# Delta net: z from PSUM by Silu, decays and key factors on ScalarE, masks on GpSimd, half of z behind the inverse's levels

## The chip, the cores and the metric

The kernel runs on one core of one Trainium2 chip. The metric is device time in microseconds from the start to the end of one execution, the median of several runs. TensorE's clock has two levels, 1.2 and 2.4 GHz; the trace gives the granted clock as 0.50 and 1.00.

## The reference

The program is a network of several layers for 256 tokens of width 1024 in fp32. The change is in its first layer, a gated delta net with 8 heads of 128:

```python
def gated_deltanet(hn, w_in, conv_w, a_log, dt_bias, out_norm_g, w_out):
    proj = hn @ w_in
    qkv = jax.nn.silu(causal_depthwise_conv(proj[..., :3 * DN_DIM], conv_w))
    z = proj[..., 3 * DN_DIM:4 * DN_DIM]
    ...
    o = chunk_gated_delta_rule(q, k, v, g, beta)
    o = rmsnorm(o, out_norm_g) * jax.nn.silu(z.reshape(b, t, DN_HEADS, DN_HEAD_DIM))
    return o.reshape(b, t, DN_DIM) @ w_out
```

Inside the chunked rule, with gc the running sum of the gates within a chunk:

```python
    decay = jnp.exp(jnp.where(tri_incl, gc[..., :, None] - gc[..., None, :], -jnp.inf))
    a_low = jnp.where(tri_strict, jnp.einsum('bhncd,bhnsd->bhncs', k_beta, k) * decay, 0.0)
    sol = lax.linalg.triangular_solve(a_mat, rhs, left_side=True, lower=True, unit_diagonal=True)
    attn_intra = jnp.einsum('bhncd,bhnsd->bhncs', q, k) * decay
    k_dec = k * jnp.exp(gc[..., -1:] - gc)[..., None]
```

The scan over chunks then makes the outputs from u, w, the decayed q and k, and attn_intra. The layers behind (an MLP, a block attention, the branch layer, its feed-forward) are the same in both kernels.

## The kernel before

A chunk here is 128 tokens, so there are 2 chunks (c) and 2 groups of 4 heads (g): four blocks (g, c), each a tile of 128 x 4 x 128. A scheduler puts every instruction into its engine's queue by priority in the order of the code; `later(n)` adds n to the priority of what stands under it, and `after(x)` (`tc.issue_after`) puts what stands under it behind instruction x on the same engine. Every engine works its queue in order.

Projections (`lin`, `group`) go in pieces of 512 columns: four weight tiles `wr` of 128x1024 come by DMA on SyncE's queue, ScalarE makes the rounded half `wh` (line 76) and VectorE the rest `wl` (line 56), and TensorE makes 96 matmuls of 128x128 on 128x256 in three passes (xh with wh, xl with wh, xh with wl) into two of the two `acc` banks of PSUM. The six other banks are `ps`. There are 4 buffers of `wr` and 5 of `wh` and `wl` each.

`delta_net` goes through these stages:

- `gates` makes beta and the running sums `gc`; `decays(g, c)` makes m = exp(-|row sum - gc|) for each block and for c = 1 the factors `qd`.
- `project` makes k, then q and vt: `conv_pair` copies the accumulator into a padded tile `pad` (its three leading columns are zeroed by GpSimd each time, line 507), starts y on ScalarE, adds three taps on VectorE (`cy`, line 59), and applies Silu.
- `unit_keys` and `gram` make the blocks of A from k, beta and m.
- `inverses`: the 32x32 diagonal blocks of A go through DRAM (`ga`, line 573; `at`, line 576; both issued by GpSimd) into a layout in which VectorE solves all of them in 31 steps of two instructions (`tmp`, `zt`). The result goes through DRAM again (`gz`, line 594; `Z`, line 597).
- `level_64` and `level_128`, each for four blocks, join the 32x32 inverses to 64x64 and then 128x128. Each has transposes (`turned`, line 603, called T below), a product with A ("Z,A"), ScalarE's copy `Y`, a product with X ("Y,X") and ScalarE's copy back into Z.
- `intra` multiplies m with the triangular mask `tri`, makes q times k ("kq" below) and multiplies it with m; for c = 1 it makes q times `qd`.
- `tokens(g)` transposes k and v, and VectorE makes kx and bv; `outputs(g)` makes u0, nw, S, vn and the outputs, normalises them and multiplies with z; the projection out follows.
- `on_z` makes Silu of z without a Silu table: a max, Exp, Ln(1+x), Exp, and a product with z and the norm's gain `onorm`. z comes in two pieces, columns 3072 to 3583 ("z0") and 3584 to 4095 ("z1").

`pin` is the load of ScalarE's table of Exp and Ln, placed behind the last Silu; what needs it stands behind it by `issue_after(pin.ins)`. Before, q and vt are written behind the levels in the code, but they and z have no need of Z and fill TensorE while VectorE works at the inverse. kq stands behind the levels, and the tokens behind kq.

Of the kernel before, what the change touches and what calls it, by code (L numbers as in the profile page):

```python
# [8 lines left out]
F32 = mybir.dt.float32  # L9
F32R = mybir.dt.float32r  # L10
I32 = mybir.dt.int32
AF = mybir.ActivationFunctionType
OP = mybir.AluOpType
# [3 lines left out]
P = 128  # L17
T = 256
D = 1024
KD = D // P  # L20
# [4 lines left out]
class Net:  # L25
# [420 lines left out]
    def delta_net(self):  # L446
        nc, tc, a = self.nc, self.tc, self.a
        W = a["dn_w_in"][0]
        H, d = 8, 128
        banks = self.ctx.enter_context(ExitStack())  # L450
        banks.enter_context(self.banks(2))
        with ExitStack() as ctx:
            dp = ctx.enter_context(tc.tile_pool(name="dn", bufs=1, reuse_waits="tile"))
# [45 lines left out]
            A = core.tile([P, 16, P], F32, name="A")  # L499
            Z = core.tile([P, 16, P], F32, name="Z")  # L500
            nc.gpsimd.memset(Z, 0.0)
            four = lambda t, g, c: t[:, (g * 2 + c) * 4:(g * 2 + c) * 4 + 4, :]

            def conv_pair(col, o, dst, behind):
                t = col // P
                pad = dp.tile([P, 2, T + 3], F32, tag="pad", name="pad", bufs=2)
                nc.gpsimd.memset(pad[:, :, 0:3], 0.0)
                self.copy(pad[:, :, 3:], o)
                y = dp.tile([P, 2, T], F32, tag="cy", name="cy", bufs=2)
                w = lambda j, i: cw[:, j * 24 + t + i:j * 24 + t + i + 1]  # L510
                for i in range(2):
                    self.act(y[:, i, :], o[:, i, :], AF.Copy, scale=w(3, i))
                for j in range(3):
                    for i in range(2):
                        self.stt(y[:, i, :], pad[:, i, j:j + T], w(j, i), y[:, i, :], OP.mult, OP.add)
                with self.after(*behind):
                    self.last_silu = self.act(dst, y, AF.Silu)
# [14 lines left out]

            def decays(g, c):

                h4 = slice(g * 4, g * 4 + 4)
                p = self.ps()
                mm4(p, lambda i: (gt[:, c, g * 4 + i:g * 4 + i + 1].to_broadcast([P, P]), self.tri[:, 0:P]))
                m = M[g, c] = big("m", 4)
                self.tt(m, v4(p), tok(gc[:, c, h4]), OP.subtract)
                if c == 1:  # L540
                    qd[g] = big("qd", 2)
                    self.last_exp = self.act(qd[g], v4(p), AF.Exp)
                self.act(m, m, AF.Abs)
                self.last_exp = self.act(m, m, AF.Exp, scale=-1.0)

            def unit_keys(g):
# [52 lines left out]
            def turned(zz):  # L599
                X = big("X", 2)  # L600
                p = self.ps()
                for i in range(4):
                    nc.tensor.transpose(p[:, i * P:(i + 1) * P], zz[:, i, :], self.ident)  # L603
                self.copy(X, v4(p))
                return X

# [32 lines left out]
            def intra(g, c):  # L639

                cs = slice(c * P, (c + 1) * P)
                m = M[g, c]
                self.tt(m, m, b4(self.tri[:, 0:P]), OP.mult)
                p = self.ps()
                mm4(p, lambda i: (k[g][:, i, cs], q[g][:, i, cs]))
                self.tt(m, v4(p), m, OP.mult)
                if c == 1:
                    self.tt(qd[g], q[g][:, :, cs], qd[g], OP.mult)

            def tokens(g):  # L650

                h4 = slice(g * 4, g * 4 + 4)
                for c in range(2):
                    cs = slice(c * P, (c + 1) * P)
                    p = self.ps()
                    for i in range(4):
                        nc.tensor.transpose(p[:, i * P:(i + 1) * P], k[g][:, i, cs], self.ident)
                    kx[c] = big(f"kx{c}", 1, late)
                    self.tt(kx[c], v4(p), tok((beg if c else kdec)[:, h4]), OP.mult)
                    p = self.ps()  # L660
                    for i in range(4):
                        nc.tensor.transpose(p[:, i * P:(i + 1) * P], vt[g][:, i, cs], self.ident)
                    bv[c] = big(f"bv{c}", 1, late)
                    self.tt(bv[c], v4(p), tok(beta[:, c, h4]), OP.mult)
# [6 lines left out]
            def outputs(g):  # L671
                Z0, Z1 = four(Z, g, 0), four(Z, g, 1)
                p = self.ps()
                mm4(p, lambda i: (Z0[:, i, :], bv[0][:, i, :]))
                u0 = big("u0", 1, late)
                self.copy(u0, v4(p))
                p = self.ps()
                mm4(p, lambda i: (kx[1][:, i, :], Z1[:, i, :]))
                nw = big("nw", 1, late)
                self.act(nw, v4(p), AF.Copy, scale=-1.0)  # L680
                yield
                p = self.ps()
                mm4(p, lambda i: (kx[0][:, i, :], u0[:, i, :]))
                S = big("S", 1, late)
                self.copy(S, v4(p))
                yield
                p = self.ps()
                for i in range(4):
                    o = p[:, i * P:(i + 1) * P]
                    self.mm(o, Z1[:, i, :], bv[1][:, i, :], i == 0, False)  # L690
                    self.mm(o, nw[:, i, :], S[:, i, :], False, True)
                vn = big("vn", 1, late)
                self.copy(vn, v4(p))
                for j in range(2):
                    yield
                    p = self.ps()
                    for i in (2 * j, 2 * j + 1):
                        o = p[:, (i % 2) * T:(i % 2) * T + T]
                        self.mm(o[:, 0:P], u0[:, i, :], M[g, 0][:, i, :], i % 2 == 0, True)
                        self.mm(o[:, P:T], S[:, i, :], qd[g][:, i, :], False, False)  # L700
                        self.mm(o[:, P:T], vn[:, i, :], M[g, 1][:, i, :], False, True)
                    o = self.pairs(p)
                    sq = self.sq_pair(o)
                    q2 = late.tile([P, 2, T], F32, tag="q2", name="q2", bufs=1)
                    self.act(q2, q[g][:, 2 * j:2 * j + 2, :], AF.Square, scale=math.sqrt(d * d * EPS))
                    self.tt(sq, sq, q2, OP.add)
                    zj = z[:, g * 4 + 2 * j:g * 4 + 2 * j + 2, :]
                    self.tt(zj, o, zj, OP.mult)
                    p = self.ps()
                    self.mm(p, self.ones, sq, True, True)  # L710
                    r = dp.tile([P, 2, T], F32, tag="kr", name="kr", bufs=1)
                    self.rsqrt_wide(r, self.pairs(p), d, oeps)
                    self.tt(zj, zj, r, OP.mult)
                    h2 = slice(2 * j, 2 * j + 2)
                    self.split(xo[g][0][:, h2, :], xo[g][1][:, h2, :], zj)

            def on_z(col, o):
                h = col // P - 24
                zj = z[:, h:h + 2, :]
                e = dp.tile([P, 2, T], F32, tag="ze", name="ze", bufs=1)  # L720
                self.ts(e, o, -80.0, None, OP.max)
                with tc.issue_after(pin.ins):
                    self.act(e, e, AF.Exp, scale=-1.0)
                self.act(e, e, AF.Ln, bias=1.0)
                self.act(e, e, AF.Exp, scale=-1.0)
                self.stt(zj, o, self.vec["onorm"], e, OP.mult, OP.mult)

            both = [(g, c) for g in range(2) for c in range(2)]
            gates()
# [11 lines left out]
            with tc.tile_pool(name="inv", bufs=1, reuse_waits="tile") as sv:  # L741
                inverses(sv)
            late = ctx.enter_context(tc.tile_pool(name="late", bufs=1, reuse_waits="tile"))
            for level in (level_64, level_128):
                for g, c in both:
                    level(four(A, g, c), four(Z, g, c))
            project(q, "q", 0, 0, behind)
            project(q, "q", 0, 1, behind)
            project(vt, "vt", 2048, 0, behind)
            project(vt, "vt", 2048, 1, behind)  # L750
            pin = self.table(self.last_silu)
            for g, c in both:
                intra(g, c)
            tokens(0)
            step = lambda it: next(it, None)
            out = [outputs(g) for g in range(2)]
            step(out[0])
            with self.later(300):
                self.lin(W, KD, [(3072, 512)], rd, on_z)
            step(out[0])  # L760
            step(out[0])
            xo[0] = (late.tile([P, 4, T], F32R, name="xoh"), late.tile([P, 4, T], F32R, name="xol"))
            with self.later(600):
                self.lin(W, KD, [(3584, 512)], rd, on_z)
            xo[1] = self.new_xg(0)
            tokens(1)
            for _ in range(6):
# [798 lines left out]
```

## Time and profile before

| | us |
|---|---|
| median of 3 runs | 1304.6 (1304.56 to 1306.42) |
| the profiled execution | 1307.26 |
| its span | 1305.5 |
| TensorE busy in the span | 1256.2 (96%) |
| VectorE, ScalarE, GpSimd busy | 866.9, 738.9, 21.1 |
| mean granted clock | 0.974 |

All times in the rows are microseconds from the start of the span, unless they are marked ns. A row of a stretch gives the busy time of each engine with its instructions, the granted clock (PEclk) and the DMA's share. The mean of a group is the modelled duration of one instruction; in a queue without waits the next begins a little before that end. A matmul's modelled duration holds its pipeline, so its price is the distance from start to start.

### The profile page before, as it was taken

To read this page: it belongs to the slowest core of one execution; us is meant where nothing else is said; L and a number is where in the kernel's file an instruction comes from. 1 tells how busy PE (TensorE), PEld (TensorE's weight loads), DVE (VectorE), ACT (ScalarE), POOL (GpSimd) and SP (SyncE) were. 2 spreads that over 40 slices of the span, in tenths; PEclk is the share of its full clock that TensorE was granted. 3 is DMA by queue.
4 is the path that set the end of the run, shared out by engine and by line. 5 is a ranking of instruction groups with operands and counts; after the bars stand their busy time and mean duration, and the time that the engine had idled before them with its cause. 6 is when DMAs were issued, how large, how long until landed. Compare 5 with 4: busy or idle time off the path is not lost.

```text
span 1305.5 us, 23759 instructions
## 1 busy us (share of the span) xinstructions
PE 1256.2 (96%) x9666; PEld 1198.3 (92%) x9666; DVE 866.9 (66%) x1385; ACT 738.9 (57%) x1126; POOL 21.1 (2%) x68
## 2 busy tenths in 40 slices
PE   7997789999999999999999999999999998999998
PEld 6997688999999999999999988799999997999997
DVE  6799236754546665744545998998556685877775
ACT  6874435654545445854545755665447565656554
POOL 2010100000000000000000000000000000000000
PEclk8998678999999999999999999999999999999999
DMA  6454302766664744656662563446564654465552
GB/s 208 136 170 146 81 1 85 238 199 184 180 191 142 216 144 146 210 163 189 180 184 78 163 178 98 145 133 192 184 187 148 206 164 129 132 207 172 183 177 83
DMA packets 99633, 207.32 MB, mean 159 GB/s; under 512 B 9694, under 2 KB 12292, under 8 KB 99524
## 3 DMA queue, kind: packets, MB, share of 16 engines
q1 hardware_dynamic: 98114, 202.85, 50.7%
q0 software_dynamic: 928, 2.88, 0.9%
q8 instruction: 76, 1.25, 0.4%
q14 instruction: 33, 0.27, 0.1%
q10 hardware_dynamic: 482, 0.08, 0.0%
HBM read 204.21 MB, written 1.57 MB: 158 GB/s over the span
## 4 chain that ended last, share of the span: by engine, by line
PE 83%; DVE 8%; ACT 3%; DMA 2%; issue 2%; POOL 0%; SPq 0%; ACTq 0%; DVEq 0%; POOLq 0%
PE acc L53 50%; PE ps L53 31%; DVE wl L56 2%; DVE yc L59 1%; ACT wh L76 1%; PE ps L603 1%; DVE cy L59 1%; PE ps L893 1%; DVE tmp L56 1%; DVE zt L56 0%; DVE sq L56 0%; DMA wr<-in_w_xkv_dram 0%; DMA Z<-gz 0%; DMA xt<-in_x_dram 0%; DMA gz<-zt 0%
## 5 line engine op out<-in xcount | busy, mean ns | idle before, releaser
L56 DVE TENSOR_TENSOR wl<-wr,wh 128x1024 fp32r<-128x1024 f32 (+1 forms) x384 | 466.5, 1219 | 304.3 <-ACT wh L76 303.3
L76 ACT ACTIVATE wh<-wr 128x1024 fp32r<-128x1024 f32 (+1 forms) x384 | 402.7, 1053 | 393.0 <-PE acc L53 241.7
L53 PE MATMUL acc<-xh,wh 128*128 128x256 f32 (+1 forms) x1064 | 306.8, 289 | 7.2 <-DVE z L59 5.2
L53 PE MATMUL acc<-xh,wl 128*128 128x256 f32 (+1 forms) x1064 | 305.7, 288 | 3.5 <-DVE wl L56 3.5
L53 PE MATMUL acc<-xl,wh 128*128 128x256 f32 (+1 forms) x1064 | 305.1, 287 | 0.8 <-DVE xl L56 0.8
L53 PE MATMUL ps<-xh,wh 128*128 128x256 f32 (+1 forms) x872 | 247.9, 285 | 6.2 <-ACT xh L69 3.5
L53 PE MATMUL ps<-xl,wh 128*128 128x256 f32 (+1 forms) x872 | 247.6, 284 | 0.5 <-DVE xl L56 0.3
L53 PE MATMUL ps<-xh,wl 128*128 128x256 f32 (+1 forms) x872 | 247.4, 284 | 0.0
L53 PEld LDWEIGHTS acc<-xh,wh 128*128 128x128 f32 (+1 forms) x1064 | 205.5, 193 | 10.8 <-issue 6.7
L53 PEld LDWEIGHTS acc<-xh,wl 128*128 128x128 f32 (+1 forms) x1064 | 205.7, 194 | 5.1 <-DVE wl L56 3.7
L53 PEld LDWEIGHTS acc<-xl,wh 128*128 128x128 f32 (+1 forms) x1064 | 206.0, 194 | 2.1 <-DVE xl L56 1.0
L53 PEld LDWEIGHTS ps<-xh,wh 128*128 128x128 f32 (+1 forms) x872 | 166.2, 191 | 7.8 <-ACT xh L69 3.9
L53 PEld LDWEIGHTS ps<-xl,wh 128*128 128x128 f32 (+1 forms) x872 | 166.3, 191 | 1.7 <-DVE xl L56 1.1
L53 PEld LDWEIGHTS ps<-xh,wl 128*128 128x128 f32 (+1 forms) x872 | 166.4, 191 | 0.3
L53 PE MATMUL acc<-hh,wh 128*128 128x256 f32 x512 | 144.6, 282 | 0.0
L53 PE MATMUL acc<-hh,wl 128*128 128x256 f32 x512 | 144.3, 282 | 0.0
L53 PE MATMUL acc<-hl,wh 128*128 128x256 f32 x512 | 144.2, 282 | 0.0
L53 PEld LDWEIGHTS acc<-hh,wl 128*128 128x128 f32 x512 | 97.3, 190 | 0.0
L53 PEld LDWEIGHTS acc<-hh,wh 128*128 128x128 f32 x512 | 97.2, 190 | 0.0
L53 PEld LDWEIGHTS acc<-hl,wh 128*128 128x128 f32 x512 | 97.1, 190 | 0.0
L59 DVE SCALAR_TENSOR_TENSOR yc<-cpad,vec_b,yc 128x256 f32<-128x256 f32 x120 | 51.3, 481 | 0.1
L59 DVE SCALAR_TENSOR_TENSOR fy<-pad,vec_b,fy 128x256 f32<-128x256 f32 x88 | 37.0, 480 | 0.1
(417 smaller groups left out, 1753.3 us busy)
## 6 DMA issues: line engine op xcount, KB each, us to landing
wr<-in_mlp_w_up_dram SPq DMA_DIRECT2D x64, 512.0 KB
wr<-in_mlp_w_down_dram SPq DMA_DIRECT2D x64, 512.0 KB
wr<-in_w_in_dram SPq DMA_DIRECT2D x44, 512.0 KB
wr<-in_w_up_dram SPq DMA_DIRECT2D x44, 512.0 KB
wr<-in_dn_w_in_dram SPq DMA_DIRECT2D x32, 512.0 KB
wr<-in_w_gate_dram SPq DMA_DIRECT2D x32, 512.0 KB
wr<-in_mb_w_in_dram SPq DMA_DIRECT2D x24, 512.0 KB
wr<-in_w_down_dram SPq DMA_DIRECT2D x22, 512.0 KB
```

Of the source, the lines that this page charges most:

```text
L53: return self.nc.tensor.matmul(out, lhsT=lhsT, rhs=rhs, start=start, stop=stop, skip_group_check=True)
L56: return (eng or self.nc.vector).tensor_tensor(out=out, in0=a, in1=b, op=op)
L59: self.nc.vector.scalar_tensor_tensor(out, a, s, b, op0=op0, op1=op1, **kw)
L76: a = self.nc.scalar.activation(hi, src, AF.Copy)
L603: nc.tensor.transpose(p[:, i * P:(i + 1) * P], zz[:, i, :], self.ident)
L893: self.nc.tensor.transpose(pt[:, i * P:(i + 1) * P], p[:, i * P:(i + 1) * P], self.ident)
```

## The change

All of it is in `delta_net`:

1. The three pads are made and zeroed once; `cy` has three buffers.
2. In `decays`, VectorE's subtraction of `gc` and ScalarE's Abs over 128x512 become four ScalarE Abs of 128x128 from PSUM, with scale -1 and `gc` as bias.
3. The product of m with `tri` goes from VectorE to GpSimd.
4. kx in `tokens` goes from one VectorE product of 128x512 to four ScalarE copies of 128x128 with a scale for each.
5. z is one Silu of ScalarE from PSUM. The gain `onorm` is multiplied in `outputs`.
6. The projections of q and vt, `intra`, and z0 are written ahead of Z's use; z1 is bound behind T of the first level (`turns[0]`) by `after`. The table load stands behind the last Silu of z, and the outputs' rsqrt behind it.

```diff
-                pad = dp.tile([P, 2, T + 3], F32, tag="pad", name="pad", bufs=2)
-                nc.gpsimd.memset(pad[:, :, 0:3], 0.0)
+                pad = pads[t // 2 % len(pads)]
...
-                self.tt(m, v4(p), tok(gc[:, c, h4]), OP.subtract)
+                for i in range(4):
+                    self.act(m[:, i, :], p[:, i * P:(i + 1) * P], AF.Abs, scale=-1.0, bias=gc[:, c, g * 4 + i:g * 4 + i + 1])
...
-                self.act(m, m, AF.Abs)
...
-                self.tt(m, m, b4(self.tri[:, 0:P]), OP.mult)
+                self.tt(m, m, b4(self.tri[:, 0:P]), OP.mult, nc.gpsimd)
...
-                    self.tt(kx[c], v4(p), tok((beg if c else kdec)[:, h4]), OP.mult)
+                    for i in range(4):
+                        h = g * 4 + i
+                        self.act(kx[c][:, i, :], p[:, i * P:(i + 1) * P], AF.Copy, scale=(beg if c else kdec)[:, h:h + 1])
...
-                    self.tt(zj, o, zj, OP.mult)
+                    self.stt(zj, o, self.vec["onorm"], zj, OP.mult, OP.mult)
...
-                e = dp.tile([P, 2, T], F32, tag="ze", name="ze", bufs=1)
-                self.ts(e, o, -80.0, None, OP.max)
-                with tc.issue_after(pin.ins):
-                    self.act(e, e, AF.Exp, scale=-1.0)
-                self.act(e, e, AF.Ln, bias=1.0)
-                self.act(e, e, AF.Exp, scale=-1.0)
-                self.stt(zj, o, self.vec["onorm"], e, OP.mult, OP.mult)
+                with self.after(*behind):
+                    self.last_silu = self.act(z[:, h:h + 2, :], o, AF.Silu)
...
+            for g, c in both:
+                intra(g, c)
+            turns = []
+            for level in (level_64, level_128):
+                for g, c in both:
+                    level(four(A, g, c), four(Z, g, c))
+                    turns.append(self.last_turn)
+            with self.later(200):
+                self.lin(W, KD, [(3072, 512)], rd, on_z)
+            with self.after(turns[0]):
+                self.lin(W, KD, [(3584, 512)], rd, on_z)
+            pin = self.table(self.last_silu)
             tokens(0)
```

The code's new order decides the queues. TensorE's queue where Z comes back, first before, then now; `ident,Z` is T, and `acc<-x.,w.` is a matmul of z:

```order
L53 MATMUL acc<-xh,wl 128x256
L603 MATMUL ps<-ident,Z 128x128 x4
L53 MATMUL ps<-Z,A 32x32 x8
L53 MATMUL ps<-Y,X 32x32 x4
L603 MATMUL ps<-ident,Z 128x128 x2
L53 MATMUL ps<-Y,X 32x32 x4
```

```order
L604 MATMUL ps<-ident,Z 128x128 x4
L53 MATMUL ps<-Z,A 32x32 x4
L53 MATMUL acc<-xh,wh 128x256
L53 MATMUL acc<-xl,wh 128x256
L53 MATMUL ps<-Z,A 32x32 x4
L53 MATMUL ps<-Y,X 32x32 x4
L604 MATMUL ps<-ident,Z 128x128 x2
L53 MATMUL ps<-Y,X 32x32 x4
```

Matmuls of z1 stand now between the two halves of "Z,A" or between "Z,A" and "Y,X": 2, 5, 6, 6, 5, 6, 4 and 4 of them in the eight levels, 38 of 96; the other 58 stand behind the last level. All 96 stood ahead of T before. kq (16 rows of `ps<-q,k`) stood behind the last "Y,X" and ahead of the tokens' transposes; it stands ahead of z0's matmuls now, and so ahead of T.

VectorE's queue where the inverse's steps begin, before and now:

```order
L56 TENSOR_TENSOR wl<-wr,wh 128x1024 x3
L56 TENSOR_TENSOR tmp<-zt,at 128x31
L56 TENSOR_TENSOR m<-m,tri 128x512
L56 TENSOR_TENSOR zt<-zt,tmp 128x31
L56 TENSOR_TENSOR m<-m,tri 128x512
L56 TENSOR_TENSOR tmp<-zt,at 128x30
L56 TENSOR_TENSOR wl<-wr,wh 128x1024
```

```order
L56 TENSOR_TENSOR wl<-wr,wh 128x1024 x2
L56 TENSOR_TENSOR tmp<-zt,at 128x31
L56 TENSOR_TENSOR wl<-wr,wh 128x1024
L56 TENSOR_TENSOR zt<-zt,tmp 128x31
L56 TENSOR_TENSOR wl<-wr,wh 128x1024
L56 TENSOR_TENSOR tmp<-zt,at 128x30
L56 TENSOR_TENSOR qd<-q,qd 128x512
```

The masks are gone from it. Between the first `tmp` and the last `zt` stood 10 `wl`, 24 `cy`, 4 masks, 2 `qd`, and of z 2 max and 2 products; now stand there 12 `wl`, 24 `cy`, 1 `qd` and the 4 products of kq with m.

ScalarE's queue behind the levels now; before, `u` followed on the last copy into Z:

```order
L69 ACTIVATE Z<-ps 64x4x64
L76 ACTIVATE wh<-wr 128x1024 x2
L69 ACTIVATE z<-acc 128x512
L76 ACTIVATE wh<-wr 128x1024
L69 ACTIVATE z<-acc 128x512
L273 ACT_TABLE_LOAD
L69 ACTIVATE kx_1840<-ps,kdec 128x128 x4
L69 ACTIVATE kx_1857<-ps,beg 128x128 x4
L72 ACTIVATE u_1874<-ps 128x512
```

The last `wh` waits for a buffer that z1's last matmul frees; both Silu of z1, the table load and kx have come in ahead of `u`.

## Rows read from the trace of the kernel before

**Rows 1.** Page, first part: engine busy us (share of the span) xinstructions

```profile
PE 1256.2 (96%) x9666; PEld 1198.3 (92%) x9666; DVE 866.9 (66%) x1385; ACT 738.9 (57%) x1126; POOL 21.1 (2%) x68
```

**Rows 2.** Stages: stretch, its length, busy us (instructions) of each engine, PEclk, DMA

```profile
60.00:86.40 26.40, 26.32 (x220) 25.91 (x219) 24.99 (x52) 19.43 (x29) 4.34 (x10) 1.00 0.62 180
86.42:130.85 44.43, 35.60 (x259) 34.64 (x258) 41.27 (x107) 23.39 (x34) 0.21 (x2) 0.88 0.45 147
130.85:145.33 14.48, 7.47 (x64) 7.30 (x62) 7.55 (x8) 7.77 (x11) 4.25 (x6) 0.86 0.73 181
145.33:173.70 28.37, 24.50 (x225) 19.38 (x225) 0.14 (x1) 11.62 (x31) 0.00 (x0) 0.50 0.01 2
173.70:180.00 6.30, 6.30 (x35) 6.30 (x35) 2.08 (x3) 0.38 (x1) 0.00 (x0) 0.59 0.00 0
180.00:222.00 42.00, 37.29 (x265) 33.31 (x264) 21.61 (x34) 20.32 (x33) 1.22 (x3) 0.93 0.19 62
```

**Rows 3.** Waits, 60 to 222 us: total us, times, longest

```profile
PE ps L603 <- DMA Z<-gz: 7.0, 1, 7.0
...
PE ps L53 <- ACT Y L72: 3.9, 8, 0.5
```

**Rows 4.** Groups on VectorE, 86.42 to 130.85 us: count, busy, mean ns, idle before

```profile
L56 DVE TENSOR_TENSOR m<-m,tri 128x512 f32<-128x512 f32 x4 | 2.7, 687 | 0.0
L59 DVE SCALAR_TENSOR_TENSOR z<-acc,vec_a,ze 128x512 f32<-128x512 f32 x2 | 1.5, 746 | 0.0
...
L64 DVE TENSOR_SCALAR ze<-acc 128x512 f32<-128x512 f32 x2 | 1.4, 689 | 2.2 <-PE acc L53 2.2
```

**Rows 5.** Groups on GpSimd, whole run

```profile
L64 POOL TENSOR_SCALAR zt<-zf 64x512 f32<-64x512 f32 x2 | 3.0, 1496 | 0.2
...
L581 POOL CAST zf<-zi 128x512 f32<-128x512 int32 x1 | 0.6, 606 | 0.1
```

**Rows 6.** Groups on ScalarE, 36 to 260 us

```profile
L76 ACT ACTIVATE wh<-wr 128x1024 fp32r<-128x1024 f32 x47 | 48.9, 1054 | 26.8 <-PE acc L53 16.6 <-DMA wr<-in_dn_w_in_dram 5.8 <-DMA vrow_b<-in_sc_w_dram 1.8
...
L69 ACT ACTIVATE m<-m 128x512 f32<-128x512 f32 x8 | 4.7, 623 | 0.9 <-DVE m L56 0.9
...
L273 ACT ACT_TABLE_LOAD x2 | 2.6, 1283 | 0.0
L69 ACT ACTIVATE q<-cy 128x512 f32<-128x512 f32 x4 | 2.5, 628 | 0.2
...
L72 ACT ACTIVATE Y<-ps 32x128 f32<-32x128 f32 x8 | 2.1, 267 | 2.9 <-PE ps L53 2.9
```

**Rows 7.** Timeline of PE and ACT: start, duration, instruction, count [idle before <-releaser]

```profile
145.33 1.09 PE L603 MATMUL ps<-ident,Z 128*128 128x128 f32 x4 [7.01 <-DMA Z<-gz]
...
179.81 0.60 PE L657 MATMUL ps<-ident,k 128*128 128x128 f32 x4
...
184.99 0.60 ACT L72 ACTIVATE S<-ps 128x512 f32<-128x512 f32 x1 [0.35 <-PE ps L53]
```

**Rows 8.** Short stretches for the clock, columns as in rows 2

```profile
4.78:8.20 3.42, 1.96 (x16) 1.49 (x14) 0.12 (x1) 2.44 (x9) 1.37 (x2) 1.00 1.09 300
8.20:11.60 3.40, 1.24 (x6) 0.79 (x6) 2.61 (x5) 1.91 (x5) 1.31 (x1) 1.00 0.61 225
114.00:117.40 3.40, 3.40 (x18) 3.40 (x17) 2.27 (x4) 1.06 (x1) 0.00 (x0) 0.50 0.91 303
124.70:127.70 3.00, 3.00 (x14) 3.00 (x15) 2.76 (x10) 1.89 (x3) 0.00 (x0) 0.51 0.88 319
127.70:131.10 3.40, 3.06 (x26) 2.88 (x26) 2.83 (x12) 0.90 (x1) 0.00 (x0) 1.00 0.02 8
148.20:158.20 10.00, 8.59 (x109) 6.62 (x108) 0.00 (x0) 4.88 (x16) 0.00 (x0) 0.50 0.01 2
158.20:173.60 15.40, 13.29 (x90) 10.75 (x88) 0.00 (x0) 5.71 (x14) 0.00 (x0) 0.50 0.01 1
175.40:178.90 3.50, 3.50 (x18) 3.50 (x18) 1.38 (x2) 0.00 (x0) 0.00 (x0) 0.51 0.00 0
```

More of the change, by code (lines that the diff above doesn't have):

```diff
@@ L501, in delta_net @@
             nc.gpsimd.memset(Z, 0.0)
+            pads = [dp.tile([P, 2, T + 3], F32, name=f"pad{i}") for i in range(3)]
+            for pad in pads:
+                nc.gpsimd.memset(pad[:, :, 0:3], 0.0)
             four = lambda t, g, c: t[:, (g * 2 + c) * 4:(g * 2 + c) * 4 + 4, :]
@@ L505, in conv_pair @@
                 t = col // P
-                pad = dp.tile([P, 2, T + 3], F32, tag="pad", name="pad", bufs=2)
-                nc.gpsimd.memset(pad[:, :, 0:3], 0.0)
+                pad = pads[t // 2 % len(pads)]
                 self.copy(pad[:, :, 3:], o)
-                y = dp.tile([P, 2, T], F32, tag="cy", name="cy", bufs=2)
+                y = dp.tile([P, 2, T], F32, tag="cy", name="cy", bufs=len(pads))
                 w = lambda j, i: cw[:, j * 24 + t + i:j * 24 + t + i + 1]
@@ L533, in decays @@
             def decays(g, c):
-                h4 = slice(g * 4, g * 4 + 4)
                 p = self.ps()
@@ L602, in turned @@
                 for i in range(4):
-                    nc.tensor.transpose(p[:, i * P:(i + 1) * P], zz[:, i, :], self.ident)
+                    self.last_turn = nc.tensor.transpose(p[:, i * P:(i + 1) * P], zz[:, i, :], self.ident)
                 self.copy(X, v4(p))
@@ L711, in outputs @@
                     r = dp.tile([P, 2, T], F32, tag="kr", name="kr", bufs=1)
-                    self.rsqrt_wide(r, self.pairs(p), d, oeps)
+                    with tc.issue_after(pin.ins):
+                        self.rsqrt_wide(r, self.pairs(p), d, oeps)
                     self.tt(zj, zj, r, OP.mult)
@@ L718, in on_z @@
                 h = col // P - 24
-                zj = z[:, h:h + 2, :]
-                e = dp.tile([P, 2, T], F32, tag="ze", name="ze", bufs=1)
-                self.ts(e, o, -80.0, None, OP.max)
-                with tc.issue_after(pin.ins):
-                    self.act(e, e, AF.Exp, scale=-1.0)
-                self.act(e, e, AF.Ln, bias=1.0)
-                self.act(e, e, AF.Exp, scale=-1.0)
-                self.stt(zj, o, self.vec["onorm"], e, OP.mult, OP.mult)
+                with self.after(*behind):
+                    self.last_silu = self.act(z[:, h:h + 2, :], o, AF.Silu)
             both = [(g, c) for g in range(2) for c in range(2)]
@@ L743, in delta_net @@
             late = ctx.enter_context(tc.tile_pool(name="late", bufs=1, reuse_waits="tile"))
-            for level in (level_64, level_128):
-                for g, c in both:
-                    level(four(A, g, c), four(Z, g, c))
             project(q, "q", 0, 0, behind)
@@ L750, in delta_net @@
             project(vt, "vt", 2048, 1, behind)
-            pin = self.table(self.last_silu)
             for g, c in both:
                 intra(g, c)
+            turns = []
[8 more added lines that the diff above has]
+            pin = self.table(self.last_silu)
             tokens(0)
@@ L756, in delta_net @@
             out = [outputs(g) for g in range(2)]
[L757 to L761, printed above, removed]
+            for _ in range(3):
+                step(out[0])
             xo[0] = (late.tile([P, 4, T], F32R, name="xoh"), late.tile([P, 4, T], F32R, name="xol"))
-            with self.later(600):
-                self.lin(W, KD, [(3584, 512)], rd, on_z)
             xo[1] = self.new_xg(0)
```

## The prediction, made before the changed kernel ran

> **What bounds the kernel now.** I read the busy shares first, then the stages around the triangular inverse, then the waits, then the groups of instructions of the stages that wait. TensorE is busy 1256.2 us of the span of 1305.5 us [rows 1], so an edit pays where TensorE idles or runs at half clock, and the delta net has both. Up to 86.4 us it is full: 220 matmuls in 26.40 us at clock 1.00, 0.120 us each [rows 2]. Then VectorE works down the 31 steps of the inverse with other work strewn between them, 41.27 us busy in 44.43 us. TensorE has matmuls to fill most of that stretch, but whatever it does there, nothing behind the inverse can begin before Z is back from DRAM: 14.48 us after the last step, TensorE's longest wait in this part being 7.0 us for that DMA [rows 2, 3]. Behind Z come the levels, 28.37 us, all at clock 0.50, and kq (q times k), 6.30 us, mostly at 0.50 [rows 2]. So the path is: VectorE to the end of the inverse, two DMA trips, levels, kq, tokens, outputs. The edits must be costed on this path alone.
>
> The profiled execution took 1307.26 us, 2.66 us above the median of 1304.6. The sum is made on 1307.26 and 2.7 is taken off at the end.
>
> **The change, part by part.**
>
> *VectorE up to the end of the inverse.* What leaves its queue between 61 us (where it becomes continuously busy) and the last step: 4 masks at 0.687, 2 max of z at 0.689, 2 products of z at 0.746; 5.6 us by durations, about 4.9 from start to start, since each next instruction begins some 0.09 us before the modelled end [rows 4]. What comes: 4 products of kq with the mask, which stood behind the levels and cost like the masks, 2.4 us start to start. Two weight splits move from ahead of the first step to behind it and one of the two qd products moves ahead of it; neither changes the sum. Net work: -2.5 us. The idle time of the stretch is 44.43 - 41.27 = 3.2 us, of which 2.2 us is the max of z waiting for its accumulation on TensorE [rows 2, 4]; that instruction is gone, but kq and the split weights can make VectorE wait instead. Ends: -5.7 (all of the idle goes) and 0 (new waits of 2.5 us together). I take half of the idle as gone, -1.5, and with ScalarE's +0.4 from below -3.6 us. The first step stays near 86 us: it can't precede the landing of `at`, whose issue now no longer waits for a pad memset, but has the fourth mask ahead of it. One cast of 128x512 took 0.606 us on GpSimd alone and a 64x512 two-scalar one 1.496 [rows 5], so the mask is 0.6 to 1.5 us, while `ga` needs longer to land; hidden. The third mask stands ahead of the `ga` DMAs and may cost 0 to 0.9.
>
> *ScalarE ahead of the inverse.* 4 Abs of 128x512 become 16 of 128x128 with a pointer. No such row exists; between the 32x128 copy at 0.267 and a quarter of the 128x512 at 0.623 (0.16) [rows 6], I take 0.25, so 4.0 against 2.5 us, while 4 VectorE subtracts on the same chain go. -1 to +2, taken +0.4, which is in the -3.6 above; the rest of it the keys' projections on TensorE hide.
>
> *Z's two trips.* Untouched, 14.48 us [rows 2]; GpSimd has no memset left between them. Z is at about 141.7 instead of 145.33 [rows 7]. From z0's end, at about 115 us, TensorE idles until then. That costs nothing in itself, because z1 is held back, but its clock is at half when Z comes, as it is before.
>
> *kq ahead of Z.* -6.30 us [rows 2], less 0.1 for its overlap with the tokens: -6.2. It is now done in time that TensorE otherwise spends waiting.
>
> *z1 behind the first transposes.* This is the payment. Its 96 matmuls cost 0.120 us each at full clock [rows 2]; at half clock 114.00:117.40 shows 16 in 3.40 us (18 touch the stretch, two at its ends), 0.213 each [rows 8]. By the order 38 of them stand in the gaps of the levels and 58 behind. In the levels TensorE was busy 24.50 of 28.37 us; the rest is the 3.9 us of eight waits for ScalarE's Y [rows 2, 3], exactly where the 38 lie. At half clock throughout the levels become 24.5 + 38 x 0.213 = 32.6 us and the 58 another 12.4: 45.0 us. If the clock returns after t, the remainder takes half: t + (45.0 - t)/2, plus some 1.5 for ScalarE's copies, which do not shrink. So t decides.
>
> Rows on t: behind 3.00 us of z's matmuls without a gap (124.70:127.70) the clock was 1.00 (127.70:131.10), and within 3.50 us of kq alone (175.40:178.90) it came back too. It did not in 148.20:158.20, TensorE busy 8.59 of 10.00, nor in 158.20:173.60, 13.29 of 15.40 [rows 8]. The gaps that held those two back are filled now, about 5 dense matmuls, 1.1 us, in each. What is left to doubt is whether transposes and 32x32 products do as much for the clock as dense ones. In 4.78:8.20 TensorE did nothing but transposes of x, 1.96 of 3.42 us, and the clock stayed at 1.00 in 8.20:11.60 [rows 8]. So transposes seem to count. I take t = 7 us, two levels: 7 + 19 + 1.5, 27.5 to 28 us. Against 28.37: -0.4.
>
> The Trainium skill, "TensorE: Matmul & The Clock Gate", Part 4 (PE-mode transpose), speaks against this edit: full clock does not engage for transposes, which don't count as busy in the same way. The stretch with transposes alone holds against it for keeping the clock (1.00 after 1.96 us of them); no row shows it for regaining it. By that rule the third rival below is the result.
>
> *Behind z1.* ScalarE has, behind z1's last matmul, a weight split whose slot only z1 frees (1.05), a Silu (0.63), the table load (1.28) and 8 pieces of kx (2.0) before it can copy u0; before, VectorE made kx, and ScalarE was free [rows 6]. The chain by hand: kx done 4.9 us behind z1, u0 copied at 5.5, S's matmuls done and its copy begun at 7.0; before, S's copy began 184.99 - 179.81 = 5.2 us behind the first transpose of the tokens [rows 7]. So +1.8 us; ends 0 (the split comes after) and +2.5. TensorE then idles some 2 us in the middle of the tokens, which may cost clock. 180 to 222 us ran at 0.93, that is 0.07 x 42 = 2.9 us lost already [rows 2]; another loss of that kind is 0 to 2.9, taken +1.0. The onorm product adds 4 x 0.06, hidden. z by Silu drops 12 ScalarE passes of 0.63 for 4; none was on the path.
>
> Sum: -3.6 - 6.2 - 0.4 + 1.8 + 1.0 = -7.4; 1307.26 - 7.4 = 1299.9; less 2.7: 1297.2 us.
>
> **The rivals.**
> 1. The clock returns only in the 64x64 levels, t about 24: 24 + 10.5 + 0.5 = 35.0 us, +6.6 instead of -0.4. 1304.2, no change. For it: 5 dense matmuls make a larger share of a 64x64 level's 4.3 us, and little of such a level is waiting; against: the 32x32 levels have no gap left either.
> 2. It changes less than it says: VectorE's new waits (kq late, a weight late) eat the 3.6 us. Then 1300.8 where the clock returns early, 1307.8 in rival 1.
> 3. Slower: half clock through all levels. 32.6 us, then the 58 dense matmuls, which bring the clock back after 3 to 5 us, as those of 124.70:127.70 did [rows 8]: 9 us. 41.5 us, +13.1, and the sum is +6.1: 1310.7. It decides from the point where levels and z1 take more than 35.4 us. For it: no row shows levels without gaps, and at 86% busy they left the clock at half through 25 us [rows 8]; against it, z's matmuls alone brought it back within 3 us. The rule of the Trainium skill on transposes ("TensorE: Matmul & The Clock Gate", Part 4) gives this time too.
>
> **How the numbers follow.** Forecast 48%, rival 1 16%, rival 2 6%, rival 3 30%. The forecast's own range is 1293 to 1301, from VectorE (-5.7 to 0 against -3.6), the tail (0 to 5.4 against 2.8) and t from 4 to 14. To hold 8 in 10 the range must reach into rival 3: 1292.5 to 1311.5 leaves out the part of it with a costly tail. This kernel's measurement tells a change of about 0.2%, 2.6 us, from none. Faster by more: 48 and half of rival 2, less 2 of the forecast's upper end: 0.49. Within: 0.17. Slower: 0.34.
>
> **What would show it.** In the levels' rows the clock: 1.00 from the second or third level on, and 28 us from the first transpose of Z to z1's last matmul; 41 us at 0.50 is rival 3. Z's wait ends near 141.7 us, the last step of the inverse near 127.2. kq's rows stand ahead of Z, none behind. ScalarE's row of kx follows a table load right behind z1, and S's copy ends 7 us after. No wait for kq or wl over 1 us on VectorE between the steps. What would make the forecast wrong first is the clock; second the end of the inverse.

## The result

| | before | changed |
|---|---|---|
| median | 1305.11 us (4 runs) | 1311.89 us (1311.19 to 1312.61, 4 runs) |
| ratio | | 1.0051, 95% interval 1.0038 to 1.0063 |
| profiled execution, its span | 1307.26, 1305.5 | 1312.51, 1310.4 |

The change made the kernel slower by half a per cent. The forecast was faster, 1297.2 us in a range up to 1311.5. The third rival (half clock through all levels, 1310.7 us) is what happened.

First the busy shares of the page of the changed kernel, then the stages (columns as in rows 2), which answer to [rows 1, 2]:

```profile
PE 1259.3 (96%) x9666; PEld 1200.1 (92%) x9666; DVE 855.7 (65%) x1365; ACT 740.2 (56%) x1146; POOL 29.4 (2%) x63
```

```profile
88.62:130.23 41.61, 31.68 (x262) 31.06 (x261) 40.50 (x104) 19.59 (x29) 0.00 (x0) 0.95 0.54 177
130.23:139.34 9.11, 0.00 (x1) 0.04 (x1) 0.00 (x0) 0.00 (x0) 4.25 (x6) 0.50 0.24 58
139.34:182.36 43.02, 43.02 (x320) 36.67 (x321) 3.68 (x3) 15.77 (x36) 0.00 (x0) 0.56 0.08 26
148.20:158.20 10.00, 10.00 (x101) 8.46 (x99) 0.00 (x0) 4.17 (x12) 0.00 (x0) 0.50 0.01 2
158.20:173.60 15.40, 15.40 (x87) 12.81 (x87) 1.22 (x1) 5.49 (x11) 0.00 (x0) 0.50 0.12 36
182.36:226.00 43.64, 38.07 (x271) 33.67 (x270) 20.35 (x31) 27.55 (x52) 1.03 (x3) 0.96 0.27 82
```

The first row is the inverse on VectorE, from its first step to its last; the second Z's two trips; the third Z's first transpose to the first transpose of the tokens. In that third row the loss lies: 43.02 us, TensorE busy for all of it, and mean clock 0.56. The next two rows are the stretches of [rows 8] in which before was busy 8.59 of 10.00 and 13.29 of 15.40 us: now 10.00 and 15.40, no gap left, and the clock still at 0.50. It came back only in z1's last block, which begins at 173.74 us:

```profile
173.60:177.00 3.40, 3.40 (x17) 3.28 (x17) 0.00 (x0) 1.31 (x2) 0.00 (x0) 0.50 0.00 0
177.20:182.36 5.16, 5.16 (x44) 5.16 (x44) 2.40 (x2) 1.66 (x2) 0.00 (x0) 0.99 0.29 102
```

The timeline around it: TensorE's first transposes of Z and of the tokens, three z1 matmuls in a level, ScalarE behind z1, and S (start, duration, instruction, count, idle before).

```profile
139.34 1.09 PE L604 MATMUL ps<-ident,Z 128*128 128x128 f32 x4 [18.29 <-DMA Z<-gz]
...
144.80 0.58 PE L53 MATMUL acc<-xh,wl 128*128 128x256 f32 x1
145.18 0.41 PE L53 MATMUL acc<-xh,wh 128*128 128x256 f32 x1
145.39 0.41 PE L53 MATMUL acc<-xl,wh 128*128 128x256 f32 x1
...
182.36 0.60 PE L658 MATMUL ps<-ident,k 128*128 128x128 f32 x4
...
183.99 1.28 ACT L273 ACT_TABLE_LOAD   x1
185.28 1.14 ACT L69 ACTIVATE kx<-ps,kdec 128x128 f32<-128x128 f32 x4
...
189.19 0.60 ACT L72 ACTIVATE S<-ps 128x512 f32<-128x512 f32 x1 [0.56 <-PE ps L53]
```

Against before [rows 7]: Z comes 145.33 - 139.34 = 6.0 us sooner, yet the tokens begin 182.36 - 179.81 = 2.55 us later and S 4.2 us later. GpSimd and VectorE ahead of the inverse:

```profile
64.80 2.99 POOL L56 TENSOR_TENSOR m<-m,tri 128x512 f32<-128x512 f32 x2 [55.51 <-DVE A L59]
72.33 1.30 POOL L56 TENSOR_TENSOR m<-m,tri 128x512 f32<-128x512 f32 x1 [4.54 <-ACT q L69]
73.56 2.85 POOL L574 DMA_DIRECT2D ga<-A  x4
76.42 5.37 POOL L56 TENSOR_TENSOR m<-m,tri 128x512 f32<-128x512 f32 x1
81.74 1.10 POOL L577 DMA_DIRECT2D at<-ga  x2
```

```profile
66.73 2.93 DVE L59 SCALAR_TENSOR_TENSOR cy<-pad,vec_a,cy 128x256 f32<-128x256 f32 x5
...
71.06 2.16 DVE L59 SCALAR_TENSOR_TENSOR A<-ps,beta,m 128x128 f32<-128x128 f32 x8
...
75.42 4.62 DVE L56 TENSOR_TENSOR wl<-wr,wh 128x1024 fp32r<-128x1024 f32 x4
...
86.35 2.34 DVE L56 TENSOR_TENSOR wl<-wr,wh 128x1024 fp32r<-128x1024 f32 x2
88.62 0.20 DVE L56 TENSOR_TENSOR tmp<-zt,at 128x31 f32<-128x31 f32 x1
```

The fourth mask took 5.37 us, 3.6 of them beside VectorE's four `wl`; the third took 1.30, most of it beside products for A that VectorE reads from PSUM. The first two ran from 64.80 to 67.79 us; the five taps that began in that time took 2.93 us.

### The profile page after: what moved, and what is told of

It is laid out like the page before. It is cut to its first block, busy times and chain, and to the rows that moved or that the text cites. A ratio compares the mean times of both kernels' runs of the same rounds, so it can differ in the third digit from the quotient of the medians.

```text
span 1310.4 us, 23733 instructions
## 1 busy us (share of the span) xinstructions
PE 1259.3 (96%) x9666; PEld 1200.1 (92%) x9666; DVE 855.7 (65%) x1365; ACT 740.2 (56%) x1146; POOL 29.4 (2%) x63
## 5 line engine op out<-in xcount | busy, mean ns | idle before, releaser
L59 DVE SCALAR_TENSOR_TENSOR cy<-pad,vec_a,cy 128x256 f32<-128x256 f32 x72 | 33.2, 500 | 9.3 <-ACT cy L69 9.2
```

The lines of the kernel that those rows point to most:

```text
L59: self.nc.vector.scalar_tensor_tensor(out, a, s, b, op0=op0, op1=op1, **kw)
```

## The experiments

Each is a variant of the changed kernel unless it says otherwise. Ratios are to the kernel before, on the same chip.

### z1 not behind the levels

```diff
-            with self.after(turns[0]):
+            with self.later(200):
                 self.lin(W, KD, [(3584, 512)], rd, on_z)
```

> The changed kernel, but z1 is not bound behind the levels' first transposes; it follows z0 at once. Theory (the payment is z1 at half clock between and behind the levels): the stretch from Z's first transpose to the tokens' transposes falls from 43.0 us to the 28.4 us of the kernel before, still at clock 0.50; the table load and both Silu of z are done early, so S comes 1.7 us sooner behind the tokens' transposes. Z's two trips may grow from 9.1 towards 14.5 us again, since z1 frees the weight buffers. So 1295 to 1301 us. Rival (the loss sits ahead of Z, in masks on GpSimd or in ScalarE's pieces): above 1307 us.

1301.72 us, 0.9963 [0.9950, 0.9976]: a little above the expected range, and faster than before. The trips, then Z to the tokens:

```profile
129.90:144.26 14.36, 3.53 (x30) 3.35 (x29) 5.96 (x6) 5.71 (x7) 4.25 (x6) 0.75 0.75 220
144.26:172.62 28.36, 24.49 (x225) 19.38 (x225) 0.00 (x0) 11.61 (x31) 0.00 (x0) 0.50 0.00 1
```

The levels are back at 28.36 us, and the loss is gone with one line: with z1 ahead, the rest of the change is a gain. The trips are back at 14.36 us: the DMA engines are busy 0.75 of the time with weights, against 0.24 in the changed kernel (9.11 us), which held z1 back and with it the weight buffers. Holding z1 back bought 5.3 us there and paid 14.7 us for it.

### z1 in one block behind the first transposes

```diff
+            X = turned(four(Z, 0, 0))
+            with self.after(self.last_turn):
+                self.lin(W, KD, [(3584, 512)], rd, on_z)
+            with self.after(self.last_mm):
                 for level in (level_64, level_128):
```

`last_mm` is the last matmul written.

> The changed kernel with one more group of four transposes of Z, then all 96 matmuls of z1 in one block, and the levels behind them. Theory (only dense matmuls bring the clock back, and the levels keep it once it is there): the block takes 13 to 15 us and ends at clock 1.00, the levels then run at 1.00 in about 17 us; 32 us instead of 43.0, so about 1301 us. Rival (the levels lose the clock again through their waits for ScalarE): 14 + 28 us, 1311 us. Rival (mixing was harmless, z1's work alone is the price): as the changed kernel, 1312 us, with 0.50 throughout.

1309.31 us, 1.0027 [1.0016, 1.0038], near the first rival. The block, the first level and a half, the rest:

```profile
139.44:153.50 14.06, 14.06 (x100) 14.06 (x101) 3.68 (x3) 4.37 (x5) 0.00 (x0) 0.83 0.27 77
153.50:158.20 4.70, 3.03 (x50) 2.35 (x48) 1.23 (x1) 4.46 (x8) 0.00 (x0) 0.96 0.53 157
158.20:181.65 23.45, 19.65 (x177) 15.87 (x177) 0.00 (x0) 9.70 (x26) 0.00 (x0) 0.50 0.04 15
```

Dense matmuls bring the clock back within the block; the levels lose it again within 5 us (mean 0.96 in the second row, 0.50 behind it). My theory that the levels keep a clock they are given is wrong. Whether their waits or their products are to blame was open: TensorE was busy 3.03 of those 4.70 us.

### z1 as a warm-up, ahead of Z

```diff
+                nc.vector.tensor_copy(probe, zt[:, 0, :])
...
+            with self.after(self.last_mm):
+                first = self.mm(p[0:32, 0:32], probe, probe, True, True)
+            with self.after(first):
+                self.lin(W, KD, [(3584, 512)], rd, on_z)
```

> The changed kernel, but z1's 96 matmuls wait for the inverse's last step (a copy of 32 columns of it feeds one small extra matmul ahead of them) and stand ahead of the levels, so that TensorE works while Z makes its two trips. Theory (the clock at Z's arrival decides the levels): z1 costs nothing on the path, the levels begin at clock 1.00 and take about 17 us instead of 43.0 with z1; 1288 to 1293 us, the upper end if weight loads slow the trips again. Rival (levels can't keep the clock): levels 28 us at 0.50, 1299 to 1302 us.

1300.03 us, 0.9953 [0.9938, 0.9968]: the rival. The first levels, then the rest:

```profile
144.35:149.40 5.05, 3.00 (x50) 2.26 (x48) 1.22 (x1) 4.80 (x10) 0.00 (x0) 0.94 0.57 178
149.50:172.42 22.92, 19.60 (x177) 15.87 (x177) 0.00 (x0) 9.28 (x25) 0.00 (x0) 0.50 0.02 6
```

### The same, with half of z1 in the gaps

48 of z1's matmuls ahead of Z, then 6 in each level between "Z,A" and "Y,X", called from the levels by `pour`:

```diff
+            pour(48)
+            with self.after(self.last_mm):
+                for level in (level_64, level_128):
...
+                pour(6)
                 p = self.ps()
```

> The changed kernel with z1 split: 48 of its matmuls wait for the inverse's last step and run while Z makes its trips (about 130.5 to 139 us, so that the clock is 1.00 when Z comes), the other 48 stand in the levels, 6 in each gap between Z,A and Y,X. Theory P (the levels lose the clock because TensorE waits for ScalarE's Y): with the gaps filled the clock stays at 1.00, the levels with 48 matmuls take 19 to 21 us, the tokens begin near 160 us, about 1288 us. Theory Q (32x32 and 64x64 products keep TensorE busy in the trace but don't count for the clock): it falls to 0.50 within the first three levels, levels and z1 take about 33 to 36 us, about 1300 us.

1308.42 us, 1.0023 [1.0013, 1.0034]; Z came 2.4 us behind the 48, and the levels ran at half from the start:

```profile
134.50:141.02 6.52, 4.12 (x35) 3.95 (x34) 2.45 (x2) 2.64 (x3) 2.60 (x4) 1.00 0.39 116
141.02:180.44 39.42, 37.55 (x272) 31.06 (x273) 1.23 (x1) 14.62 (x35) 0.00 (x0) 0.50 0.09 29
```

Since Z was late, this run doesn't part the two theories on losing the clock. It does show once more that levels with six dense matmuls in each gap don't bring it back. The next runs take the kinds of matmul one by one.

### Transposes as ordinary matmuls

```diff
-                    self.last_turn = nc.tensor.transpose(p[:, i * P:(i + 1) * P], zz[:, i, :], self.ident)
+                    self.last_turn = self.mm(p[:, i * P:(i + 1) * P], zz[:, i, :], self.ident, True, True)
```

> The changed kernel with the levels' transposes made as ordinary matmuls with the identity (each takes about twice as long). Theory of the Trainium skill's page on TensorE, Part 4 (transposes don't count as work for the clock): with z1 between, the clock now returns early in the levels, 43 + 6.6 us at half become about 30, so about 1299 us. Rival (the 32x32 and 64x64 products are what doesn't bring the clock back, or both): the clock stays at 0.50 and the longer transposes cost 6 to 7 us, about 1318 us.

1320.78 us, 1.0114 [1.0099, 1.0129], the rival with a little more:

```profile
138.82:185.00 46.18, 46.18 (x305) 39.98 (x306) 1.22 (x1) 13.11 (x34) 0.00 (x0) 0.50 0.04 13
```

With no transpose left in the levels, and z1 between, the clock stayed at 0.50; it came back at about 186 us, again in z1's last block, and the tokens began at 191.12, 52.3 us behind Z. The transposes are not what holds it down. That they bring it back can be seen in the run with z1 in one block: behind its levels, at 0.50, stand the 16 transposes of the tokens and nothing else, and then the products:

```profile
181.65:185.00 3.35, 3.35 (x17) 3.35 (x17) 0.69 (x1) 2.01 (x7) 0.00 (x0) 0.50 0.00 0
185.10:188.00 2.90, 2.90 (x28) 2.90 (x27) 0.69 (x1) 1.74 (x5) 0.00 (x0) 1.00 0.00 0
```

After 3.4 us of transposes alone the clock was 1.00.

### Three kinds, one after the other

```diff
+                for i in range(54):
+                    t = nc.tensor.transpose(p[:, i % 4 * P:i % 4 * P + P], one, one)
...
+                for i in range(44):
+                    t = self.mm(p[0:64, i % 8 * 64:i % 8 * 64 + 64], one[0:64, 0:64], one[0:64, 0:64], True, True)
...
+                for i in range(110):
+                    t = self.mm(p[0:32, i % 16 * 32:i % 16 * 32 + 32], one[0:32, 0:32], one[0:32, 0:32], True, True)
```

> The changed kernel with 54 transposes of 128x128, then 44 products of 64x64, then 110 of 32x32, all of the constant identity and read by nobody, in the 18 us in which TensorE waits for Z behind z0. No waits between them. Theory Q: the clock stays at 1.00 through the transposes (6 us) and falls to 0.50 in the 64x64 products or in the 32x32 ones, although TensorE is busy all the time. Theory of the Trainium skill's page (transposes don't count): it falls already in the transposes. Theory P (only waits matter): it stays at 1.00 to the end, Z's levels begin at 1.00. The time itself should move by less than 4 us against the changed kernel's 1312 (a product or two may still be in TensorE's queue when Z comes).

One execution, 1313.32 us. Four stretches: transposes; 64x64 products; 15 records of 64x64 and then 79 of 32x32; 32x32 alone. Behind them the two groups of that stretch of products.

```profile
120.60:126.50 5.90, 5.90 (x55) 5.76 (x53) 5.56 (x13) 2.06 (x3) 0.00 (x0) 1.00 0.95 323
126.60:130.90 4.30, 4.30 (x76) 4.30 (x76) 3.04 (x14) 0.00 (x0) 0.52 (x1) 1.00 0.42 128
131.00:134.30 3.30, 3.30 (x94) 3.23 (x93) 0.00 (x0) 0.00 (x0) 1.03 (x2) 1.00 0.37 84
134.60:141.80 7.20, 7.20 (x139) 7.20 (x137) 0.00 (x0) 0.00 (x0) 2.60 (x4) 0.50 0.15 39
```

```profile
L53 PE MATMUL ps<-ident 32*32 32x32 f32 x220 | 10.2, 220 | 0.0
L53 PE MATMUL ps<-ident 64*64 64x64 f32 x88 | 5.3, 219 | 0.0
```

TensorE is busy without a gap for 21 us, and the clock falls to 0.50 at 134.4 us, some 2.7 us into the 32x32 products. 5.9 us of transposes alone left it at 1.00, and so did 5.3 us of 64x64 products. So a waiting TensorE isn't needed to lose the clock: it fell among 32x32 products at 100% busy. It is one execution in one order; whether the 64x64 products just ahead have a part in the fall it can't tell.

### Full products instead of small ones

If the products are to blame, larger ones must mend it, although they are more work. In the changed kernel:

```diff
-                for r in (0, 64):
-                    for i in range(4):
-                        self.mm(p[r:r + 32, i * 32:(i + 1) * 32], A[r + 32:r + 64, i, r:r + 32],
-                                zz[r + 32:r + 64, i, r + 32:r + 64], True, True)
-                    self.copy(Y[r:r + 32, :, 0:32], v(p, r))
+                mm4(p, lambda i: (A[:, i, :], zz[:, i, :]))
+                self.copy(Y, v4(p))
```

> The changed kernel with every 32x32 and 64x64 product of the levels made as a 128x128 one (the blocks outside are multiplied by zeros of Z, and only the same blocks are copied out); more work for TensorE: 8 matmul records of 0.23 us at half clock instead of 0.05 or 0.13. Theory Q (small products don't count for the clock): the clock returns to 1.00 within the first two or three levels, Z's first transpose to the tokens takes 32 to 36 us instead of 43.0, 1302 to 1306 us. Rival (the clock needs something else, such as no change of operand types): half clock throughout, 43 + 13 us, about 1325 us.

1301.75 us, 0.9976 [0.9967, 0.9985]. From Z on:

```profile
139.35:143.60 4.25, 4.25 (x20) 4.25 (x21) 0.00 (x0) 1.20 (x2) 0.00 (x0) 0.50 0.02 4
143.70:172.80 29.10, 28.86 (x237) 27.46 (x237) 3.68 (x3) 15.80 (x30) 0.00 (x0) 1.00 0.11 37
```

More arithmetic, and 10 us less: the clock is back 4.3 us behind Z, 33.5 us to the tokens (172.84 - 139.35) instead of 43.0. z1 is bound as before, but 47 of its matmuls stand in the gaps now instead of 38, five or six in each. That isn't what brought the clock back: the run above with six in every gap, between small products, stayed at 0.50. So the small products are what held the clock at half.

Only the 32x32 ones made full, in the kernel with z1 as warm-up:

> The kernel with z1 behind the inverse's last step and ahead of the levels (z1_warm), with the 32x32 products alone made as 128x128 ones. Theory Q with 32x32 alone to blame: the clock stays at 1.00 through the first four levels and, since 64x64 products held it in the test of kinds, through the others too; levels 23 to 25 us instead of 28.1, about 1296 us against z1_warm's 1300. Rival (64x64 products with their waits lose it too): 1.00 for four levels, then 0.50; 12 + 15 us, no gain.

1296.32 us, 0.9932 [0.9917, 0.9947], as theory Q had it. The four levels with full products, the four with 64x64:

```profile
144.96:158.20 13.24, 9.90 (x82) 9.13 (x81) 1.23 (x1) 8.99 (x17) 0.00 (x0) 1.00 0.26 80
158.25:167.80 9.55, 7.43 (x80) 6.01 (x79) 0.00 (x0) 5.50 (x13) 0.00 (x0) 0.97 0.00 0
```

The 64x64 levels hold the clock for some 9 us, with TensorE busy 7.43 of 9.55, and lose it just at their end; whether by their waits or by their products stays open. Holding is not regaining: in the changed kernel the 64x64 levels (157.03 to 173.74 us), without a gap and with z1 between, stayed at 0.50.

### A version that beats both

The levels as generators, so that the next level's transposes and "Z,A" stand ahead of the last one's "Y,X":

```diff
+                for n in (32, 64):
+                    for g, c in both:
+                        now = level(four(A, g, c), four(Z, g, c), n)
+                        next(now)
+                        if last:
+                            next(last, None)
+                        last = now
```

> z1_warm with all products of the levels as 128x128 and the next level's transposes and first product written ahead of the last level's second product, so that no wait for ScalarE is left between them. Theory Q: clock 1.00 from Z to the tokens, 8 levels of 2.3 us, 18 to 20 us instead of 28.1; about 1291 us, below both kernels. Rival (clock lost although all products are full): 38 us at half, 1310 us.

1289.67 us, 0.9880 [0.9864, 0.9897].

```profile
144.69:162.86 18.17, 18.17 (x162) 18.01 (x161) 1.23 (x1) 14.97 (x30) 0.00 (x0) 1.00 0.18 59
```

And with the kernel before, where only the levels are made so and z stays:

> The kernel before with nothing changed but its levels: all products 128x128, the next level's transposes and first product ahead of the last one's second product. Theory Q (the clock follows what the products are, not where z stands): the levels begin at 0.50, the clock returns within 4 to 7 us, levels 21 to 23 us instead of 28.4 and kq 3.7 instead of 6.3; about 1296 us. Rival (the edits of the change are needed for it, by warming TensorE ahead of Z): half clock throughout, 38 us, 1315 us.

1294.86 us, 0.9916 [0.9899, 0.9932]. The first levels, the others, kq:

```profile
145.62:151.30 5.68, 5.68 (x32) 5.68 (x33) 0.75 (x1) 3.06 (x6) 0.00 (x0) 0.61 0.01 3
151.40:165.60 14.20, 14.20 (x129) 14.16 (x128) 0.00 (x0) 10.44 (x23) 0.00 (x0) 1.00 0.00 1
165.70:169.27 3.57, 3.57 (x34) 3.57 (x33) 2.07 (x3) 0.38 (x1) 0.00 (x0) 1.00 0.02 5
```

Full products bring the clock back without any dense z1; 10 of the 15 us were to be had by a change of the levels alone.

### Two parts by themselves

The masks back on VectorE (`nc.gpsimd` taken out of `intra`):

> The changed kernel with the product of m and the triangular mask back on VectorE. In the changed kernel the fourth mask took 5.37 us on GpSimd and stood ahead of the DMAs of the inverse's input; five taps of the convolution beside a mask took 2.93 us on VectorE instead of 2.06. Theory (the masks on GpSimd hold the inverse's start and slow VectorE, and so ate the gain that was forecast): the first step comes 2 us sooner, VectorE has 2.4 us more to do, the last step moves by -1 to +1 us; the time stays within 2 us of 1311.9. Rival (the masks on GpSimd are a gain as forecast): the last step comes 2.5 us later, 1314.5.

1313.57 us, 1.0060 [1.0045, 1.0075]. The inverse's first and last step:

```profile
86.07 0.21 DVE L56 TENSOR_TENSOR tmp<-zt,at 128x31 f32<-128x31 f32 x1
...
132.25 0.19 DVE L56 TENSOR_TENSOR zt<-zt,tmp 128x16 f32<-128x16 f32 x1
```

The first step comes 2.5 us sooner than in the changed kernel (88.62), the last 2.2 us later (130.04 there): on GpSimd the masks make the stretch of steps 4.8 us shorter and its start 2.5 later. On the last step the rival is right, and they are a gain of 2.2 us there. The medians' intervals, 1.0038 to 1.0063 and 1.0045 to 1.0075, overlap.

The kernel before with q, vt and `intra` written ahead of the levels, and nothing else:

> The kernel before with one change of order: the block of q, vt, masks and kq is written ahead of the levels, z stays as it was. Theory (kq's 6.3 us at half clock leave the path): 1305.5 - 6.3, about 1299.3 us, with Z's first transpose where it was (145 us). Rival (kq's products with m on VectorE delay the inverse's last step by 2.4 us): 1301.7 us.

1304.00 us against 1304.42, 0.9997 [0.9987, 1.0007]: no change, neither of the two; a gain of over 1.7 us is outside the interval. In its profiled execution the inverse's last step comes 1.6 us later (132.28 against 130.66 us), as the rival has it, and Z 0.5 us later (145.80). The tokens do begin earlier, at 175.63 us instead of 179.81. But they begin at half clock, which kq had ended before:

```profile
175.63:181.52 5.89, 5.89 (x43) 5.89 (x43) 2.67 (x4) 1.57 (x3) 0.00 (x0) 0.80 0.00 0
```

From there to S it takes 5.89 us instead of 5.18, so that S comes 3.5 us earlier. And that execution took 1302.58 us, 1.4 us below its median, and the one of before was 2.7 us above its own; the two differences together are 4.1 of the 4.7 us between them. Where the executions of one kernel part by some microseconds no run showed, so what kq ahead is worth stays open; the 6.3 us that were expected of it are not borne out.

## Why the prediction was wrong

By its own terms, the forecast beside what the profiled executions show (their spans differ by 4.9 us, the medians by 6.8):

| term | forecast | measured |
|---|---|---|
| last step of the inverse | -3.6 | 130.23 against 130.85: -0.6 |
| Z's trips | 0 | 9.11 against 14.48: -5.4 |
| kq off the path | -6.2 | 173.70 to 179.81 gone from its place: -6.1; as a gain not shown (no change by itself) |
| levels and z1 | -0.4 | 43.02 against 28.37: +14.7 |
| Silu, table load and kx ahead of u0 | +1.8 | 6.83 against 5.18 from the tokens' transposes to S: +1.65 |
| clock behind | +1.0 | none lost: 0.96 in 182.36:226.00 against 0.93 in 180:222; +0.7 is left of the span's +4.9, its cause open |

**The step that failed is t.** I took the clock to return 7 us behind Z, once the gaps were filled; it returned only in z1's last block, behind the last level, 38 us behind Z, held down by the small products of the levels and not by gaps: with full products it was back after 4.3 us. The working of levels and z1 at half clock held: 41.5 us against 43.02 measured, and the third rival at 1310.7 against 1311.89. That its total came so near is in part luck: Z's trips were 5.4 us shorter than it has them, the last step 3.0 us later. The extra 1.5 us are in the levels, 34.4 us (139.34 to 173.74) against 32.6; at least part of that goes with mixing: z1's first matmul in a gap holds TensorE for 0.38 us (144.80 to 145.18) where the next takes 0.21, in eight gaps.

The row that should have warned me stood in front of me. 158.20:173.60 was 86% busy at half clock, and z's matmuls brought the clock back at 124.70:127.70 [rows 8]. I read the difference as one of gaps. It was one of kinds (124.70:127.70 are dense matmuls, 158.20:173.60 mostly 64x64 products and transposes), and the prediction said that this was in doubt, but then doubted the wrong kind: it looked at the transposes, for which the trace had a row (4.78:8.20), and let the 32x32 products, for which it had none, follow them. The bound for what has no row is both ends, and t should have been either 7 or the whole stretch with equal chance.

The Trainium skill, "TensorE: Matmul & The Clock Gate", Part 4, gave the right time by a reason that the runs don't bear out here: its rule that transposes don't count as busy stands against 5.9 us of transposes at clock 1.00, and against the clock's return behind 3.4 us of transposes alone (185 us in the run with z1 in one block). And half clock without any transpose in the levels shows that another cause is enough.

**The inverse's start.** The removal from VectorE's queue was right in size: first to last step 41.61 us instead of 44.43. But the first step came at 88.62 instead of 86.42. I hid the masks on GpSimd behind the DMA of `ga` at 0.6 to 1.5 us each. Beside VectorE's `wl` one took 5.37, so that the `at` DMAs were issued at 81.74. But `at` did not set the start (before, they were issued at 81.16): the first step stands straight behind a `wl` on VectorE, without idle time, in both kernels. It is VectorE's own queue that was late, in good part because VectorE was slower beside masks: five taps 2.93 us, against 2.06 for five in the kernel before.

```profile
72.06 2.06 DVE L59 SCALAR_TENSOR_TENSOR cy<-pad,vec_a,cy 128x256 f32<-128x256 f32 x5
...
85.27 1.23 DVE L56 TENSOR_TENSOR wl<-wr,wh 128x1024 fp32r<-128x1024 f32 x1 [0.23 <-ACT wh L76]
86.42 0.21 DVE L56 TENSOR_TENSOR tmp<-zt,at 128x31 f32<-128x31 f32 x1
```

Against the run with the masks on VectorE the same taps and one product for k took 2.1 us longer in all between 62 and 87 us (2.93 for 2.07, 1.08 for 0.68, 2.35 for 2.06, 5.40 for 4.84).

The rows I bounded the mask by [rows 5] are of operations with one input, so 1.5 us was no upper bound. Part of the later start, 0.9 us, was there ahead of the new Abs (ScalarE made `beg` at 35.95 us instead of 35.05); no run tells whether the new pads or the spread of executions made it. The Trainium skill has this one ("GPSIMD Engine Reference", section 8: its SBUF interfaces are shared with VectorE, with contention when a VectorE instruction has two SBUF inputs), the numbers above agree with it, and I had not used it.

**The trips.** I left them at 14.48 us and didn't ask what else used the DMA engines in them. Binding z1 kept its weights in the buffers, so SyncE had nothing to load: share 0.24 instead of 0.73, 5.4 us less. The run with z1 ahead gave it back (0.75, 14.36 us). This gain hid part of the loss: with trips as before the change would have cost some 5 us more, by an estimate from these rows.

Right were the tail (+1.65 against +1.8), ScalarE's 16 pieces as hidden (the sums of squares of k came at 48.32 us instead of 47.42, the same 0.9 later as `beg`), and kq's place, though not its worth.

## What to carry to other kernels

A busy share alone doesn't tell the clock: ask what kind of matmul makes it up, and test a doubtful kind by itself in a stretch where TensorE has nothing to do. Where small products hold the clock at half, full ones on zero blocks can be faster although they are several times the work (here 10 us), and should be tried before dense work is moved between them. Work that is held back also holds back its buffers and DMAs, so that transfers beside it get faster; price both sides.

## What the hardware showed that I had not expected

- Among 32x32 products the clock fell to 0.50 with TensorE busy 100% (at 134.4 us in the test of kinds), while 128x128 transposes (5.9 us) and 64x64 products (5.3 us) left it at 1.00. Transposes alone brought it back from 0.50 in 3.4 us (181.65 to 185 us in the run with z1 in one block).
- Six dense matmuls of 128x256 in each of the eight levels didn't bring it back in 39 us; with 128x128 products instead of the small ones it was back in 4.3 us.
- A 128x512 product on GpSimd took 1.30 us beside VectorE's products out of PSUM and 5.37 us when most of it ran beside four 128x1024 differences of VectorE, which kept their speed (4.62 us for four, as without the mask); beside VectorE's taps it was the taps that lost (2.93 us for five against 2.06).
